# Attention stage of an encoder trunk: the bias kept as loaded, the far probabilities' parts moved forward, the weights' and keys' parts moved between the two heads' copies of values

## The chip, the cores and the metric

The kernel runs on one core of a Trainium2 chip. A core has five engines that run their own instruction streams and meet at semaphores: TensorE (PE in the profile, its weight loads PEld), VectorE (DVE), ScalarE (ACT), GpSimd (POOL) and SyncE (SP, which here only issues DMAs). Products of TensorE land in PSUM, eight banks of 512 f32 columns by 128 partitions; everything else lives in SBUF, 128 partitions wide. The metric is the device time of one execution in microseconds, taken as the median of several runs. Lower is better.

## The reference

One layer over 1024 tokens of width 1024, all in f32. What matters here is the attention between the input projection and the output projection:

```python
hn = rmsnorm(h, norm_mix_g[i])
z = hn @ w_in[i]
u = z[..., :POOL_W]                          # 512 columns for the pooling mixer
q, k, v = jnp.split(z[..., POOL_W:], 3, axis=-1)   # 8 heads of 64
a = pool_mixer(u, pool_w[i], pool_b[i], pool_scale[i])
o = chunk_attention(q, k, v, rel_bias[i])
h = h + jnp.concatenate([a, o], axis=-1) @ w_out[i]

# chunk_attention, for each chunk of 64 tokens: own chunk and the 8 before it
s = jnp.einsum('bqhd,bkhd->bhqk', qb, kb).astype(jnp.float32) * scale + bias
s = jnp.where(valid[None, None, None, :], s, -jnp.inf)
pr = jax.nn.softmax(s, axis=-1).astype(vb.dtype)
return jnp.einsum('bhqk,bkhd->bqhd', pr, vb)
```

After it come a gated MLP with a causal convolution, a gated per-layer embedding and a final norm; the change does not touch them.

## The kernel before

TensorE's fast format holds fewer bits than f32, so each f32 matrix is split into a high part (rounded, written by ACT: `act.activation(hi, src, AF.Copy)`) and a low part (what is left, written mostly by DVE: `src - hi`), and each product is three matmuls: high by high, high by low, low by high (`mm3`, lines 136 to 138). Whatever TensorE multiplies must first have gone through ACT and then DVE or POOL.

**Units.** The attention is cut into units: one pair of heads and one tile of 128 query tokens, except that the first three tiles go together. Four pairs by six units make 24 units (`UNITS`, numbered u). A query tile sees at most five key tiles. `unit(u)` issues the work of a unit in this order:

- `probs_t(u - 1)`: TensorE turns the probabilities of the unit before (L421) into PSUM banks 2 and 3; what does not fit there goes to banks 6 and 7. The parts of banks 2 and 3 are the near ones, those of 6 and 7 the far ones (`far = bank > 3`).
- `scores(u)`: queries by keys (L398) into banks 4 to 7.
- some steps of the projections (`fill`): 24 matmuls in all for a block of 128 columns, half the tokens and all eight slices of depth, three for each step. They keep TensorE busy while the other engines do the softmax. They make the next pair's queries and keys and, after those, the columns of the pooling mixer.
- `values(u - 1)`, if that unit closed one of the groups of tiles 0 to 2, 3 to 5 and 6 to 7: probabilities by values (L473) for both heads of the pair, in 12, 24 and 24 matmuls. With a group of three tiles each head has a PSUM bank of its own (bank 5 and the projection's free bank); with the group of two both heads share one. ACT then copies a half of each head's result (L476) and DVE adds the other half (L479). A unit with such a call is called valued.

**The order on ACT and DVE** is written out by hand through a list. `push(t, f)` puts a piece of work on the list with a due time in microseconds from the unit's start; `flush()` sorts the list by due time and issues everything. Both engines then run their instructions in the order issued. The due times that matter here: near high part 0.0, first reduction (L363, L367: scores plus bias, and the row's extreme) 1.0 and 1.8, exponentials (L375) 1.9 and 2.75, near low part 2.5 in a valued unit and 3.7 otherwise, reciprocals (L378) about 2.95 to 3.5, far high part 3.5, scalings (L373 on DVE, L371 on ACT) 3.0 to 4.0, far low part 3.55 or 4.4, the copy-out of a finished projection (L279, L559) when its matmuls are issued, at 3.6 at the earliest in a unit that is not valued. At 4.8 and later come the parts of the next pair's keys and queries (`lay`, L308 to L312) and of the projections' weights (`split_later`, L504 and L502; some low parts go to POOL).

```python
            flush()
            if u:
                values(u - 1)
```

So before the change all of a unit's work is issued before its products with the values are copied out. The weights go through two buffers of raw f32 (`load`, L190) and three slots of parts; the last block's two halves have places of their own. The first of the output projection's raw weights are loaded (L615) into the same raw buffers, each as soon as the input weights there have been split.

**The bias** of a head is a 128 by 640 tile, loaded (L348) into one of three buffers while the pair before is worked on. The queries carry the factor -1/8, so that a row's minimum is wanted, and the bias is negated by ACT after it has landed (L351); POOL then fills two corners with a large number that masks keys outside the band (L352, L353).

After the last unit come the rest of the projection, the output weights' parts and the parts of the attention's result (L141 and L142 through `split`), then the output projection and the mixer. ACT's and DVE's instructions of this part have an order of their own, and the program merges the two orders by its own estimate of when each is ready.

Of the kernel before, what the change touches and what calls it, by code (L numbers as in the profile page):

```python
# [11 lines left out]
P = 128  # L12
# [89 lines left out]
def trunk(tc, xT, pT, vecs, w_qk0, w_in, w_v, bias, counts, pool_w, w_out, w_up, w_down,  # L102
# [4 lines left out]
    with tc.tile_pool(name="sb", bufs=1) as sb, \  # L107
# [175 lines left out]

        def push(t, *fns):

            for n, fn in enumerate(fns):
                pending.append((t + 0.8 * n, len(pending), fn))

        def flush():
            todo = sorted(pending, key=lambda p: p[:2])  # L290
            pending.clear()
            owed.clear()
            for _, _, fn in todo:
                fn()


        def lay(c, x, h):

            z = slice(h * 512, (h + 1) * 512)

            def last(fn):
                fn()
                laid.add((c, x, h))

            src = qk32[x][:, z]
            if x:
                hi, lo = [a[:, z] for a in K[c % 2]]
                return [lambda: act.activation(hi, src, AF.Copy),  # L308
                        lambda: last(lambda: dve.tensor_tensor(lo, src, rv(hi), ALU.subtract))]
            hi, lo = [a[:, z] for a in Q]  # L310
            return [lambda: act.activation(hi, src, AF.Copy, scale=-0.125),
                    lambda: last(lambda: dve.scalar_tensor_tensor(lo, src, -0.125, rv(hi), ALU.mult, ALU.subtract))]  # L312

# [32 lines left out]
        def load_bias(h):  # L346
# [3 lines left out]
            def turned():  # L350
                act.activation(b, b, AF.Copy, scale=-1.0)  # L351
                pool.memset(b[0:64, 576:640], BIG)  # L352
                pool.memset(b[64:128, 0:64], BIG)  # L353
            return turned

        def softmax(todo, valued):

            for i, (x, b, ps, S, s_) in enumerate(todo):
                z = 2 * i / len(todo)

                def least(b=b, ps=ps, S=S, s_=s_):
                    if len(ps.shape) == 3:
                        dve.tensor_tensor_reduce(  # L363
                            S.rearrange("p (a b) -> p a b", a=2), ps,
                            b.rearrange("p (a b) -> p a b", a=2), 1.0, BIG, ALU.add, ALU.min, s_[:, 0:1])
                    else:
                        dve.tensor_tensor_reduce(S, ps, b, 1.0, BIG, ALU.add, ALU.min, s_[:, 0:1])  # L367

# [65 lines left out]
        def probs_out(todo, valued):  # L434
            for a, b, bank, ps in todo:
                src = ps.rearrange("p a (n q) -> p n a q", q=HD)
                hi, lo = [pt[:, a:b].rearrange("p k x (a q) -> p (k x) a q", a=2) for pt in PT]
                far = bank > 3
                push(3.5 if far else 0.0, lambda hi=hi, src=src: act.activation(hi, src, AF.Copy))
                push((3.55 if valued else 4.4) if far else 2.5 if valued else 3.7,  # L440
                     lambda lo=lo, src=src, hi=hi: dve.tensor_tensor(lo, src, rv(hi), ALU.subtract))
# [3 lines left out]
        def values(u):  # L445
# [6 lines left out]
            while u < NU - 1 and at[0] < 2.3:  # L452
                next(fill)
                credit -= 0.5
                now[0] += STEP
            flush()
            reach = {k: (max(t0, k), min(t1, k + BANDT)) for k in range(max(0, t0 - 4), t1)}
# [17 lines left out]
            for j in range(2):  # L475
                act.activation(otmp[halves[j], 0:n * P], Os[j][halves[1 - j]], AF.Copy)  # L476
            for j in range(2):
                a = halves[j]
                dve.tensor_tensor(o32[a, c_, t0 * P:t1 * P], Os[j][a], otmp[a, 0:n * P], ALU.add)  # L479

# [16 lines left out]
        def split_later(parts):  # L497

            t = max(5.2, now[0] + 0.4)
            for i, (name, src, hi, lo) in enumerate(parts):  # L500
                def low(name=name, src=src, hi=hi, lo=lo):
                    (pool if name[0] in (4 + 1, 8 + 2, 4 + 2, 8 + 3, 2) else dve).tensor_tensor(lo, src, rv(hi), ALU.subtract)  # L502
                    there.add(name)
                push(t + 0.7 * i, lambda src=src, hi=hi: act.activation(hi, src, AF.Copy))  # L504
                push(t + 0.8 + 0.7 * i, low)

# [140 lines left out]
        def lay_due(u):  # L647

            for c, x, h in list(qk_ready):
                if u >= (c - 1) * PER + (0 if x else PER - 1 if h else 1):  # L650
                    qk_ready.remove((c, x, h))
                    push(max(4.8, now[0] + 0.4), *lay(c, x, h))

# [3 lines left out]
        def unit(u):  # L657
# [33 lines left out]
            else:  # L691
                for _ in range(DRAIN):
                    now[0] += STEP
                    next(fill)
            flush()
            if u:
                values(u - 1)
            if turns and (u % PER == PER - 1 or u % PER == 1):
# [767 lines left out]
```

## Time and profile before

| | |
|---|---|
| time, median of 3 runs | 1122.74 us (1122.15 to 1123.06) |
| time of the profiled execution | 1122.08 us |
| its span, first to last instruction | 1120.3 us |
| busy: PE, DVE, ACT, POOL | 99%, 76%, 52%, 15% |
| mean granted clock of TensorE | 0.998 |
| attention stage | about 80 to 262 us |

Times in the profile are counted from the span's start. A row of the timeline has the start, the length, the engine, the line, the operation, what it writes and reads, its shape, how many like it are joined, and in brackets the idle time of its engine just before it with what ended it. A matmul's length in such a row includes its way through the array: matmuls of 512 columns start 0.23 us apart and are shown as 0.39 us long.

### The profile page before, as it was taken

What the parts mean: (1) busy time and instruction counts of PE and PEld (TensorE: products, weight loads), DVE (VectorE), ACT (ScalarE), POOL (GpSimd) and SP (SyncE); (2) the same over time, 40 slices, a digit from 0 to 9 for tenths busy, and PEclk for the clock granted to TensorE, in tenths of its full rate; (3) what the DMA queues carried; (4) which work ended last, traced back from release to release, by engine and by line L of the source; (5) the groups of instructions that cost most, each with busy time, mean ns of one, the idle gap of its engine ahead of it and who ended that gap; (6) DMA issues with size and microseconds to landing.
All of it is one profiled execution on the core that took longest, in us unless ns stands there. A gap on an engine that the chain in (4) does not pass through costs nothing.

```text
span 1120.3 us, 15614 instructions
## 1 busy us (share of the span) xinstructions
PE 1108.7 (99%) x5674; PEld 921.3 (82%) x5674; DVE 850.7 (76%) x1438; ACT 581.7 (52%) x1006; POOL 167.9 (15%) x212
## 2 busy tenths in 40 slices
PE   9999999999999999999999999999999999999997
PEld 7888888888888888888888888888888888888887
DVE  7537777778578878887787878777877789986845
ACT  8336777765665545443443444344544444674634
POOL 0000101186013200220121012201120112000000
PEclk9999999999999999999999999999999999999999
DMA  8100111104600452764567456756575556420003
GB/s 308 50 1 20 62 43 39 51 16 136 197 29 1 109 155 95 164 156 140 150 160 168 133 160 151 172 138 160 142 174 145 137 156 140 132 94 20 1 34 117
DMA packets 64878, 124.83 MB, mean 111 GB/s; under 512 B 7329, under 2 KB 8737, under 8 KB 64801
## 3 DMA queue, kind: packets, MB, share of 16 engines
q1 hardware_dynamic: 50688, 98.33, 26.8%
q0 software_dynamic: 13824, 25.17, 14.2%
q8 instruction: 44, 0.72, 0.3%
q10 hardware_dynamic: 288, 0.33, 0.1%
q14 instruction: 34, 0.27, 0.1%
HBM read 109.13 MB, written 14.68 MB: 111 GB/s over the span
## 4 chain that ended last, share of the span: by engine, by line
PE 65%; DVE 3%; issue 2%; ACT 1%; POOL 1%; POOLq 0%; DVEq 0%; ACTq 0%
PE PS L136 21%; PE PS L137 21%; PE PS L138 21%; DVE R L142 1%; ACT R L141 1%; POOL TB L925 0%; POOL F L915 0%; DVE F L907 0%; DVE F L1191 0%; ACT TB L896 0%; PE PS L778 0%; POOL small L782 0%; ACT F L770 0%; DVE TB L918 0%; DVE TB L919 0%
## 5 line engine op out<-in xcount | busy, mean ns | idle before, releaser
L136 PE MATMUL PS<-R 128*128 128x512 f32 (+1 forms) x1088 | 422.2, 388 | 0.2
L137 PE MATMUL PS<-R 128*128 128x512 f32 (+1 forms) x1088 | 418.7, 385 | 0.0
L138 PE MATMUL PS<-R 128*128 128x512 f32 (+1 forms) x1088 | 418.5, 385 | 0.0
L136 PEld LDWEIGHTS PS<-R 128*128 128x128 f32 x1088 | 204.6, 188 | 44.6 <-issue 2.9
L138 PEld LDWEIGHTS PS<-R 128*128 128x128 f32 x1088 | 204.5, 188 | 41.3
L137 PEld LDWEIGHTS PS<-R 128*128 128x128 f32 x1088 | 204.6, 188 | 39.8 <-DVE R L249 0.2
L141 ACT ACTIVATE R<-F 128x512 fp32r<-128x512 f32 (+2 forms) x221 | 137.4, 636 | 177.1 <-PE PS L137 85.6
L142 DVE TENSOR_TENSOR R<-F,R 128x512 fp32r<-128x512 f32 (+2 forms) x221 | 154.5, 713 | 49.7 <-ACT R L141 49.0
L1160 DVE TENSOR_TENSOR F<-F,PS 128x512 f32<-128x512 f32 x140 | 92.6, 681 | 6.8 <-PE PS L138 6.5
L850 DVE TENSOR_TENSOR F<-F 128x512 f32<-128x512 f32 x88 | 60.5, 688 | 44.8 <-DMA F<-in_w_up 42.1
L141 ACT ACTIVATE BQ<-RW 128x512 fp32r<-128x512 f32 x90 | 52.6, 622 | 80.4 <-PE PS L137 76.3
L1103 POOL DMA_DIRECT2D RW<-Yd x56 | 49.5, 889 | 264.4 <-DMA RW<-Yd 200.8
L1103 POOL DMA_DIRECT2D RW<-in_w_down x40 | 36.5, 966 | 228.7 <-DMA RW<-in_w_down 191.1
L142 DVE TENSOR_TENSOR BQ<-RW,BQ 128x512 fp32r<-128x512 f32 x90 | 59.1, 684 | 2.6 <-PE PS L137 2.2
L137 PE MATMUL PS<-BQ 128*128 128x512 f32 x140 | 54.6, 390 | 0.1
L136 PE MATMUL PS<-R,BQ 128*128 128x512 f32 x140 | 54.5, 389 | 0.0
L138 PE MATMUL PS<-R,BQ 128*128 128x512 f32 x140 | 54.5, 389 | 0.0
L136 PE MATMUL PS<-BQ 128*128 128x512 f32 x140 | 54.5, 389 | 0.0
L137 PE MATMUL PS<-R,BQ 128*128 128x512 f32 x140 | 54.5, 389 | 0.0
L138 PE MATMUL PS<-BQ 128*128 128x512 f32 x140 | 54.5, 389 | 0.0
L986 ACT ACTIVATE F<-F,vec 128x1024 f32<-128x1024 f32 (+1 forms) x25 | 28.6, 1143 | 44.1 <-DVE F L961 41.9
L375 ACT ACTIVATE F<-F,small 128x640 f32<-128x640 f32 (+4 forms) x64 | 44.0, 689 | 14.0 <-DVE small L363 12.6
(177 smaller groups left out, 1589.7 us busy)
## 6 DMA issues: line engine op xcount, KB each, us to landing
F<-in_w_up SPq DMA_DIRECT2D x91, 256.0 KB, 4.3
RW<-Yd SPq DMA_DIRECT2D x60, 256.0 KB, 3.8
RW<-Yd POOLq DMA_DIRECT2D x56, 256.0 KB, 4.9
RW<-in_w_down SPq DMA_DIRECT2D x50, 256.0 KB, 2.9
RW<-in_w_down POOLq DMA_DIRECT2D x40, 256.0 KB, 6.6
Yd<-F SPq DMA_DIRECT2D x40, 256.0 KB, 3.1
F<-in_w_in SPq DMA_DIRECT2D x10, 512.0 KB, 3.5
F<-in_xT SPq DMA_DIRECT2D x16, 256.0 KB, 5.4
```

Of the source, the lines that this page charges most:

```text
L136: pe.matmul(ps, ahi, bhi, start=first, stop=False, skip_group_check=more)
L137: pe.matmul(ps, ahi, blo, start=False, stop=False, skip_group_check=more)
L138: pe.matmul(ps, alo, bhi, start=False, stop=last, skip_group_check=more)
L141: both = (act.activation(hi, src, AF.Copy), dve.tensor_tensor(lo, src, rv(hi), ALU.subtract))
L142: dve.tensor_tensor(lo, src, rv(hi), ALU.subtract))
L375: push(1.9 + 0.85 * z, lambda S=S, s_=s_: act.activation(S, S, AF.Exp, bias=s_[:, 0:1], scale=-1.0, accum_out=s_[:, 1:2]))
L850: return dve.tensor_tensor(rawu[to], rawu[a], rawu[b], op)
L986: act.activation(y, Gb[:, 2 + a:2 + b], AF.Identity, bias=vec[:, C_CB + fi:C_CB + fi + 1], scale=cw(2))
L1103: pool.dma_start(t, src, accum_op=ALU.add)
L1160: dve.tensor_tensor(t, t, PS[:, 4 + d], ALU.subtract if n in (1, 5) else ALU.add)
```

## The change

Four things are done:

- The queries carry +1/8, the reduction multiplies by -1, and the bias stays as loaded. The negations on ACT (L351) are gone. The two corners are filled by DVE and with the opposite sign; POOL no longer takes part.
- The far high part is due at 0.05 and not 3.5, so behind the near high part; the far low part is due right behind the near low part (2.52 in a valued unit, 3.57 otherwise), which puts it ahead of reciprocals and scalings in a valued unit and ahead of the projection's copy-out in the others.
- Work of `split_later` and `lay_due` is marked slow. In a valued unit the list is first issued without the slow work (`flush(True)`), then come the products with the values. For a group of three tiles the slow work is issued between the first head's copy and addition and the second's. For the group of two it is issued after both.
- For a group of three tiles the order copy, copy, addition, addition becomes copy, addition, (slow work,) copy, addition on the list; for the group of two it stays.

```diff
@@ -281,17 +281,17 @@
         laid = set()
         pending, now, owed = [], [0.0], set()
 
-        def push(t, *fns):
+        def push(t, *fns, slow=False):
 
             for n, fn in enumerate(fns):
-                pending.append((t + 0.8 * n, len(pending), fn))
-
-        def flush():
-            todo = sorted(pending, key=lambda p: p[:2])
-            pending.clear()
+                pending.append((t + 0.8 * n, len(pending), fn, slow))
+
+        def flush(part=False):
+            todo = sorted((p for p in pending if not (part and p[3])), key=lambda p: p[:2])
+            pending[:] = [p for p in pending if part and p[3]]
             owed.clear()
-            for _, _, fn in todo:
-                fn()
+            for p in todo:
+                p[2]()
 
 
         def lay(c, x, h):
@@ -308,8 +308,8 @@
                 return [lambda: act.activation(hi, src, AF.Copy),
                         lambda: last(lambda: dve.tensor_tensor(lo, src, rv(hi), ALU.subtract))]
             hi, lo = [a[:, z] for a in Q]
-            return [lambda: act.activation(hi, src, AF.Copy, scale=-0.125),
-                    lambda: last(lambda: dve.scalar_tensor_tensor(lo, src, -0.125, rv(hi), ALU.mult, ALU.subtract))]
+            return [lambda: act.activation(hi, src, AF.Copy, scale=0.125),
+                    lambda: last(lambda: dve.scalar_tensor_tensor(lo, src, 0.125, rv(hi), ALU.mult, ALU.subtract))]
 
         later, tail = [], []
 
@@ -348,9 +348,8 @@
             sp.dma_start(b, bias[h])
 
             def turned():
-                act.activation(b, b, AF.Copy, scale=-1.0)
-                pool.memset(b[0:64, 576:640], BIG)
-                pool.memset(b[64:128, 0:64], BIG)
+                dve.memset(b[0:64, 576:640], -BIG)
+                dve.memset(b[64:128, 0:64], -BIG)
             return turned
 
         def softmax(todo, valued):
@@ -362,9 +361,9 @@
                     if len(ps.shape) == 3:
                         dve.tensor_tensor_reduce(
                             S.rearrange("p (a b) -> p a b", a=2), ps,
-                            b.rearrange("p (a b) -> p a b", a=2), 1.0, BIG, ALU.add, ALU.min, s_[:, 0:1])
+                            b.rearrange("p (a b) -> p a b", a=2), -1.0, BIG, ALU.add, ALU.min, s_[:, 0:1])
                     else:
-                        dve.tensor_tensor_reduce(S, ps, b, 1.0, BIG, ALU.add, ALU.min, s_[:, 0:1])
+                        dve.tensor_tensor_reduce(S, ps, b, -1.0, BIG, ALU.add, ALU.min, s_[:, 0:1])
 
                 def scaled(x=x, S=S, s_=s_):
                     if x:
@@ -436,8 +435,8 @@
                 src = ps.rearrange("p a (n q) -> p n a q", q=HD)
                 hi, lo = [pt[:, a:b].rearrange("p k x (a q) -> p (k x) a q", a=2) for pt in PT]
                 far = bank > 3
-                push(3.5 if far else 0.0, lambda hi=hi, src=src: act.activation(hi, src, AF.Copy))
-                push((3.55 if valued else 4.4) if far else 2.5 if valued else 3.7,
+                push(0.05 if far else 0.0, lambda hi=hi, src=src: act.activation(hi, src, AF.Copy))
+                push((2.5 if valued else 3.55) + 0.02 * far,
                      lambda lo=lo, src=src, hi=hi: dve.tensor_tensor(lo, src, rv(hi), ALU.subtract))
 
         credit, turns, valued = 0.0, [], [False]
@@ -453,7 +452,7 @@
                 next(fill)
                 credit -= 0.5
                 now[0] += STEP
-            flush()
+            flush(True)
             reach = {k: (max(t0, k), min(t1, k + BANDT)) for k in range(max(0, t0 - 4), t1)}
             wide = [k for k, (a, b) in reach.items() if b - a == n]
             narrow = sorted((k for k in reach if k not in wide), key=lambda k: reach[k][1] - reach[k][0])
@@ -473,10 +472,15 @@
                     pe.matmul(Os[j][:, (a - t0) * P:(b - t0) * P].rearrange("p (t q) -> p t q", q=P), V[:, k, 2 * c_ + j],
                               PT[part][:, b0:b0 + by * (b - a - 1) + 1:by, j], start=n_ == 0, stop=n_ == len(todo) - 1)
             for j in range(2):
-                act.activation(otmp[halves[j], 0:n * P], Os[j][halves[1 - j]], AF.Copy)
-            for j in range(2):
                 a = halves[j]
-                dve.tensor_tensor(o32[a, c_, t0 * P:t1 * P], Os[j][a], otmp[a, 0:n * P], ALU.add)
+                act.activation(otmp[a, 0:n * P], Os[j][halves[1 - j]], AF.Copy)
+                if n == 2 and j == 0:
+                    continue
+                for i in range(2) if n == 2 else (j,):
+                    a = halves[i]
+                    dve.tensor_tensor(o32[a, c_, t0 * P:t1 * P], Os[i][a], otmp[a, 0:n * P], ALU.add)
+                if j == 0:
+                    flush()
 
         nw = [0]
         bankn = [0]
@@ -501,8 +505,8 @@
                 def low(name=name, src=src, hi=hi, lo=lo):
                     (pool if name[0] in (4 + 1, 8 + 2, 4 + 2, 8 + 3, 2) else dve).tensor_tensor(lo, src, rv(hi), ALU.subtract)
                     there.add(name)
-                push(t + 0.7 * i, lambda src=src, hi=hi: act.activation(hi, src, AF.Copy))
-                push(t + 0.8 + 0.7 * i, low)
+                push(t + 0.7 * i, lambda src=src, hi=hi: act.activation(hi, src, AF.Copy), slow=True)
+                push(t + 0.8 + 0.7 * i, low, slow=True)
 
         def weights(ct, half):
 
@@ -649,7 +653,7 @@
             for c, x, h in list(qk_ready):
                 if u >= (c - 1) * PER + (0 if x else PER - 1 if h else 1):
                     qk_ready.remove((c, x, h))
-                    push(max(4.8, now[0] + 0.4), *lay(c, x, h))
+                    push(max(4.8, now[0] + 0.4), *lay(c, x, h), slow=True)
 
         for h in range(3):
             load_bias(h)()
@@ -692,9 +696,10 @@
                 for _ in range(DRAIN):
                     now[0] += STEP
                     next(fill)
+            if valued[0]:
+                flush(True)
+                values(u - 1)
             flush()
-            if u:
-                values(u - 1)
             if turns and (u % PER == PER - 1 or u % PER == 1):
                 turns.pop(0)()
             run_later(LATER)
```

## The prediction

> **What bounds the kernel now.** I read the page first, then the instructions of TensorE in order of time through the attention stage (80 to 262 us), then those of ScalarE (ACT) and VectorE (DVE) beside them.
>
> ```profile
> span 1120.3 us, 15614 instructions
> ...
> PE   9999999999999999999999999999999999999997
> ...
> PEclk9999999999999999999999999999999999999999
> ```
>
> TensorE is busy in all 40 slices at the full granted clock, so the time is TensorE's own stream plus the places where that stream stands still. This change touches no matmul and, as I follow the planner, not their order either. It can only remove or add standstills. These rows show the products with the values (L473), one call each; a row that goes on unbroken is a call without a wait, and in brackets stands what ended a wait.
>
> ```profile
> 85.89 1.79 PE L473 MATMUL PS<-B,R 128*128 128x384 f32 x12
> 149.07 3.66 PE L473 MATMUL PS<-B,R 128*128 128x384 f32 x24
> 166.78 2.96 PE L473 MATMUL PS<-B,R 128*128 128x256 f32 x24
> ...
> 104.06 1.33 PE L473 MATMUL PS<-B,R 128*128 128x384 f32 x7
> 105.68 2.70 PE L473 MATMUL PS<-B,R 128*128 128x128 f32 x17 [0.29 <-DVE B L441]
> 119.92 0.51 PE L473 MATMUL PS<-B,R 128*128 128x256 f32 x3
> 122.39 2.02 PE L473 MATMUL PS<-B,R 128*128 128x128 f32 x15 [0.46 <-DVE B L441]
> 195.07 1.32 PE L473 MATMUL PS<-B,R 128*128 128x384 f32 x7
> 196.68 2.71 PE L473 MATMUL PS<-B,R 128*128 128x128 f32 x17 [0.29 <-DVE B L441]
> 210.94 3.12 PE L473 MATMUL PS<-B,R 128*128 128x256 f32 x24
> 219.18 0.73 PE L473 MATMUL PS<-B,R 128*128 128x384 f32 x4
> 220.67 1.31 PE L473 MATMUL PS<-B,R 128*128 128x128 f32 x8 [0.76 <-DVE B L441]
> ...
> 159.04 0.92 PE L421 MATMUL PS<-ident,F 64*128 64x64 f32 x20 [0.33 <-DVE B L441]
> 249.65 0.59 PE L421 MATMUL PS<-ident,F 64*128 64x64 f32 x12 [0.46 <-DVE B L441]
> ```
>
> The first three rows are undisturbed calls of the three kinds: 1.79 us (tiles 0 to 2), 3.66 us (tiles 3 to 5), 2.96 us (tiles 6 and 7). Against them the call at 104.06 ends at 108.38, 4.32 us, so 0.66 us is lost; the one at 195.07 ends at 199.39, again 0.66 lost; 119.92 to 124.41 is 4.49 us, 1.53 lost; 210.94 loses 0.16; 219.18 to 221.98 is 2.80 us, 1.01 lost. Two runs of transposes (L421) waited 0.33 and 0.46 us. All of it together is 4.8 us, 0.4% of the time: more than that this change cannot give here.
>
> **The change part by part.**
>
> *Far parts behind near ones.* The probabilities of the last one or two key tiles (the far ones) come out as a high part on ACT (L439) and a low part on DVE (L441).
>
> ```profile
> 103.42 1.22 DVE L441 TENSOR_TENSOR B<-PS,B 128x1024 fp32r<-128x1024 f32 x1
> 105.20 0.42 DVE L441 TENSOR_TENSOR B<-PS,B 128x256 fp32r<-128x256 f32 x1
> L375 ACT ACTIVATE F<-F,small 128x640 f32<-128x640 f32 x32 | 26.3, 824 | 10.6 <-DVE small L363 10.6
> 219.06 0.96 DVE L373 TENSOR_SCALAR F<-F,small 128x512 f32<-128x512 f32 x1
> ```
>
> The wait of the call at 104.06 ended with the far low part, 105.20 to 105.62, which stood behind two reciprocals and a scaling. It now follows the near low part (103.42 to 104.64) directly and is done at about 105.0, when the products come to it (the eighth of 24, each 0.15 us: 104.06 + 1.0). The 0.66 goes, twice. The calls at 210.94 and 219.18 waited for the same part (in the latter case also behind the projection's copy-out): 0.16 and 1.01 go. At 159.04 and 249.65 the far low part stood behind a copy-out that now comes after it: 0.33 and 0.46 go. What the far high part costs ahead of the exponentials (0.36 us on ACT) is hidden: ACT idles 10.6 us before the 32 wide exponentials, two to a unit, 0.66 a unit, waiting for DVE; in the two tightest units about 0.1 us is left over, and falls on DVE work that has 0.3 us to spare. The scalings come 0.4 us later in units with values; the next transposes start two or more microseconds after them, but for the unit at 219, below.
>
> *Bias as loaded.* Eight negations leave ACT and sixteen fills move from POOL to DVE; the sign moves into constants that the reductions and the queries' parts carry already, at no cost.
>
> ```profile
> 117.64 0.29 DVE L367 CUSTOM_DVE_ANT_0 F<-PS,F 128x128 f32<-128x128 f32 x1 [1.07 <-POOL F L352]
> L219 DVE MEMSET B<- x1: 485/485/485, 0.9 to 0.9; 128x512 f32 x1
> ```
>
> The first row is where it pays: DVE stood 1.07 us for POOL's fill, which came behind the negation and behind a 1.28 us subtraction of a weight. With that gone, and the far part forward, the products at 119.92 find everything ready: the whole 1.53 goes. Of DVE fills the trace has one of 512 columns, 0.485 us; one of 64 costs between an eighth of it, 0.06, and the whole. I take 0.1, as the length goes with the columns in the copies too, so 0.2 us a head. The loads land before DVE comes to them, as the bias of heads 3 and 4 was asked for at 111 us and is filled at about 116.
>
> So the gains are 0.66 + 0.66 + 1.53 + 0.16 + 1.01 + 0.33 + 0.46 = 4.8 us.
>
> *Weights' and keys' parts between the copies of values.* Here the change adds waits. Before, these parts (ACT L504, L308, L311; low parts on DVE or POOL) ran while ACT had nothing to do but wait for the products. Now they are queued behind the copy L476 of the first head, which waits for the products, and ahead of that of the second.
>
> ```profile
> 176.92 0.62 ACT L504 ACTIVATE R<-F 128x512 fp32r<-128x512 f32 x1
> 177.91 0.49 ACT L476 ACTIVATE F<-PS 64x384 f32<-64x384 f32 x1 [0.38 <-PE PS L473]
> 178.73 0.48 ACT L476 ACTIVATE F<-PS 64x384 f32<-64x384 f32 x1 [0.33 <-PE PS L473]
> 180.31 0.82 DVE L363 CUSTOM_DVE_ANT_0 F<-PS,F 128x640 f32<-128x640 f32 x1 [0.50 <-PE PS L398]
> 183.02 1.21 DVE L441 TENSOR_TENSOR B<-PS,B 128x1024 fp32r<-128x1024 f32 x1
> 184.51 0.84 PE L421 MATMUL PS<-ident,F 64*128 64x64 f32 x20
> ```
>
> After the long calls (1.8 us from one head's copy to the other's) the parts fit between. After the short ones they do not. In this unit three copies of 0.52 each, start to start, now stand between 178.40 and the second copy: it begins at 180.1 and not 178.73. The addition and the two fills follow, and DVE's first reduction for the next tile starts at 181.35 instead of 180.31. That tile's chain (reduction, two exponentials, reciprocal, near low part 183.02 to 184.23) has only 0.28 us before the transposes at 184.51: TensorE waits 0.8 us. The unit at 131 us has two such copies, not three, so 0.5 less: 0.25. The one at 219 has one, but the unit before it now ends with its weight copy behind both value copies, so its chain runs 0.5 us late; the far part and the projection's copy-out (1.3 us together) now stand before its scaling too, which goes from 219.06 to about 220.05 and lasts 0.96 us beside POOL: 221.0. The products, freed of their wait, end at 220.74: the transposes wait 0.3. The first head's copy comes behind ACT's scaling, its addition ends at 221.9, and the scores want that bank at 221.55: 0.35 more. So 0.65 here. The unit at 86 us has one copy and 0.8 us of slack: nothing. Sum 1.7; between 0.5 (if fills and additions overlap what I put behind each other) and 2.5 (a second copy's 0.5 more in two units).
>
> The loads of input weights (L190) are issued when a weight's low part frees their buffer, so they too go up to 2.5 us later; each is first split more than a unit (6 us) after it has landed, so nothing waits.
>
> After tiles 6 and 7 both copies come first and the parts after them. That is harmless where the weights are needed a unit later, and only pushes the next unit's first copies back by 0.5 us (counted above where it tells). In the last call they are needed at once:
>
> ```profile
> 251.40 0.63 ACT L504 ACTIVATE B<-F 128x512 fp32r<-128x512 f32 x1
> 255.35 0.68 DVE L502 TENSOR_TENSOR B<-F,B 128x512 fp32r<-128x512 f32 x1
> 256.05 0.33 SPq L615 DMA_DIRECT2D F<-in_w_out  x1
> 256.44 2.96 PE L473 MATMUL PS<-B,R 128*128 128x256 f32 x24
> 258.99 2.72 ACT L141 ACTIVATE R<-F 128x512 fp32r<-128x512 f32 x5 [5.16 <-DMA F<-in_w_out]
> 259.24 0.40 PE L136 MATMUL PS<-R,B 128*128 128x512 f32 x1
> 261.74 0.77 ACT L476 ACTIVATE F<-PS 64x256 f32<-64x256 f32 x2
> ...
> 169.77 0.77 ACT L476 ACTIVATE F<-PS 64x256 f32<-64x256 f32 x2 [2.72 <-PE PS L473]
> ...
> 264.54 0.85 DVE L479 TENSOR_TENSOR F<-PS,F 64x256 f32<-64x256 f32 x2
> 233.91 1.22 DVE L502 TENSOR_TENSOR B<-F,B 128x512 fp32r<-128x512 f32 x1
> ```
>
> The last half of the last projection's weights is made at 251.40 and 255.35, and TensorE uses it at 259.24, right behind the last products. Now it is flushed behind both copies of these products. Those can start 2.99 us after the call begins (169.77 against 166.78), so at 259.43; they take 0.77, the weight's high part 0.63 more: 260.85, where TensorE wanted it at 259.24, 1.6 us. The low part follows on DVE behind two additions (0.85) and the high part, and takes 0.68 us, or 1.22 as at 233.91 if POOL is busy beside it: 261.7 to 262.2, while the third matmul wants it at 261.4: 0.3 to 0.8 more. I take 2.2 (1.9 to 2.4), nearer to the slow row since POOL is still pooling there. Zero is the lower end, if ACT's order differs from what I read. The load of the next output weights (256.05, issued when the weight's low part freed its buffer) moves to 262 too, and with it the five copies that begin at 258.99: they and their low parts (4.95 us on DVE before, behind them the pooled parts) come some 3.5 us late against TensorE. By my reading of DVE's queue up to 287 us the mixer's last product still finds its parts with 0.5 us to spare.
>
> Behind 262 us nothing removes what is left; TensorE's stream runs on without a gap, so it goes into the time whole. Sum: 4.8 gained, 1.7 and 2.2 lost, net 0.9. The profiled execution took 1122.08 us (span 1120.3 and 1.8 around it), 0.66 under the median of 1122.74; the same subtraction from the median gives **1121.8 us**.
>
> One question remains, whether a standstill of 2.2 us costs the clock too.
>
> ```profile
> 1.49 3.78 PE L221 MATMUL PS<-B 128*128 128x512 f32 x8 [1.49 <-DVE B L219]
> ```
>
> The first eight matmuls take 3.78 us where later ones of that size follow every 0.23 us, though the page rounds that slice to full clock; no wait in the attention stage, the longest 0.76 us, lowered it. I take no loss. The Trainium skill, "TensorE: Matmul & The Clock Gate", section "What's actually happening", has the clock fall to half after an idle window of about 3.4 us; by that 2.2 us of standstill is too short and the sum stays 1121.8, while the 3.9 us of the fourth rival below would be long enough. No run here shows such a fall.
>
> **The rivals.**
>
> *The last wait is hidden (17%).* If the last weight's parts land ahead of the products' copies, only the 1.7 is lost: 1122.7 - 3.1 = 1119.6. For it: before, copies of later work (258.99) stand between earlier ones, so the order on ACT is not purely the written one. Against: that is a merge of two lists, and inside the first the copies come first.
>
> *No part waits (5%).* All 4.8 are kept: 1117.9. Against it, the 0.28 us of slack at 184.51.
>
> *The late chain reaches the mixer (12%).* The weight loads, five copies and their low parts take more than the 0.5 us to spare; a load that takes 1 to 2 us longer gives 1122.8 to 1123.8.
>
> *The five copies stay ahead (7%), slower.* If ACT keeps 258.99's five copies in front, the value copies end at 262.51, the weight's high part at 263.15, the additions at 265.39, its low part at 266.1. TensorE stands 3.9 and then 2.5 us, 6.4 instead of 2.2: 1126.0, slower than before by 3.3. It decides as soon as the last wait passes 3.1 us. Against it: the first of the five needs a load into the buffer that this very weight occupies. If the clock then also fell, 2 us more (the first eight matmuls' 3.78 against 8 x 0.23).
>
> **How the numbers follow.** The sum holds within 1120.4 and 1122.8 with 55%; clock and what I have not seen get 4%. 0.2% (2.25 us) is about what a measurement of this kernel can tell from no change. The likeliest case lies within it, as does the late chain: same 0.65. Faster takes the first two rivals and the fast end of the sum, 0.26; slower the last rival and the rest, 0.09. The range, 1119.0 to 1124.3, takes in the hidden last wait below and the late chain above.
>
> **What would show it.** Right: calls of 3.66, 2.96 and 1.79 us throughout; no wait of DVE for POOL's fill near 117; transposes waiting 0.2 to 0.8 us after the short calls of the second and third head pair; a wait of TensorE of 1.9 to 2.4 us, ended by L504's and L502's writes, behind the last products. Wrong: no wait there, or one of over 3 us; transposes at 184 on time; new waits of the mixer's products.

## The result and the profile after

The changed kernel takes 1130.17 us (median of 6 runs, 1128.84 to 1130.91), the kernel before 1122.16 on the same chip (6 runs, 1121.73 to 1123.06): ratio 1.0068, 95% interval 1.0055 to 1.0081. It is 8.0 us slower, where 0.9 less was forecast. The profiled execution took 1130.05 us, span 1128.3. From the page of the kernel after, its span and the row of the granted clock (the row of TensorE's busy share reads as before):

```profile
span 1128.3 us, 15594 instructions
...
PEclk9999999999999999999999999999999999999998
```

At this scale next to nothing has changed, which is why the stage has to be opened. TensorE in order of time, the rows that answer to those of the prediction (line numbers have moved by a few: L472 are the products with the values, L420 the transposes, L362 and L366 the reductions, L438 and L440 the high and low parts of the probabilities, L508 and L506 those of the weights, L476 the copies of values, L481 their additions):

```profile
86.53 2.18 PE L472 MATMUL PS<-B,R 128*128 128x384 f32 x12
101.22 0.92 PE L420 MATMUL PS<-ident,F 64*128 64x64 f32 x20 [0.62 <-DVE B L440]
105.85 4.09 PE L472 MATMUL PS<-B,R 128*128 128x384 f32 x24
121.77 2.96 PE L472 MATMUL PS<-B,R 128*128 128x256 f32 x24
130.53 2.12 PE L472 MATMUL PS<-B,R 128*128 128x384 f32 x12
139.41 0.84 PE L420 MATMUL PS<-ident,F 64*128 64x64 f32 x20 [0.42 <-DVE B L440]
146.34 0.92 PE L420 MATMUL PS<-ident,F 64*128 64x64 f32 x20 [0.84 <-DVE B L440]
...
170.27 3.03 PE L472 MATMUL PS<-B,R 128*128 128x256 f32 x24 [0.93 <-ACT F L370]
188.97 0.84 PE L420 MATMUL PS<-ident,F 64*128 64x64 f32 x20 [0.83 <-DVE B L440]
195.37 0.92 PE L420 MATMUL PS<-ident,F 64*128 64x64 f32 x20 [0.33 <-DVE B L440]
```

The call at 121.77 is clean (2.96 us; before, 4.49): that gain came. The calls at 86.53 and 130.53, clean before, now take 2.18 and 2.12 in place of 1.79. The waits at 139.41 and 188.97 are the forecast ones; those at 101.22, 146.34 and 195.37 are new and stand where no part between copies can have made them. The transposes wait for the near low part each time, so it is the chain ahead of it that is late. What that chain waits for stands in the groups of VectorE's instructions from 84 to 262 us (busy time and mean | idle time just before them and what ended it), first of the kernel before, then after, and in its total of waits after (us, times, longest):

```profile
L363 DVE CUSTOM_DVE_ANT_0 F<-PS,F 128x640 f32<-128x640 f32 (+1 forms) x38 | 29.0, 801 | 10.3 <-PE PS L398 9.9
```

```profile
L362 DVE CUSTOM_DVE_ANT_0 F<-PS,F 128x640 f32<-128x640 f32 (+1 forms) x39 | 29.7, 799 | 17.1 <-ACT B L438 16.6 <-PE PS L397 0.5
...
DVE F L362 <- ACT B L438: 16.6, 15, 2.0
```

Before, the reduction waited for the scores on TensorE. Now it waits, 15 times, for the high parts on ACT, and 6.8 us longer in all. One unit of each, ACT and VectorE in order of time, before and after:

```profile
100.33 1.03 ACT L439 ACTIVATE B<-PS 128x1024 fp32r<-128x1024 f32 x1 [0.84 <-PE PS L421]
101.32 0.82 DVE L363 CUSTOM_DVE_ANT_0 F<-PS,F 128x640 f32<-128x640 f32 x1 [1.77 <-PE PS L398]
102.19 0.83 ACT L375 ACTIVATE F<-F,small 128x640 f32<-128x640 f32 x1 [0.83 <-DVE small L363]
```

```profile
102.12 1.38 ACT L438 ACTIVATE B<-PS 128x1024 fp32r<-128x1024 f32 x2 [0.69 <-PE PS L420]
103.53 0.82 DVE L362 CUSTOM_DVE_ANT_0 F<-PS,F 128x640 f32<-128x640 f32 x1 [2.04 <-ACT B L438]
104.40 0.83 ACT L374 ACTIVATE F<-F,small 128x640 f32<-128x640 f32 x1 [0.90 <-DVE small L362]
```

Near and far copy now follow each other (102.12 to 103.50), and the reduction starts 0.03 us after the far one ends: 1.41 us after the near copy began, where it was 0.99. So it is 0.42 us late against the near copy, and the exponentials with it. In the unit before, that distance grew from 0.39 us to 1.31, by 0.92. The reduction takes no data from this copy. They have the banks in common: by the code the far parts lie in banks 6 and 7 beside the scores (`place`: bank 6 from column 512 down), and a tile of over three key tiles has its scores in banks 4 + x and 6 + x. The compiled order of VectorE's instructions, with what each waits for, shows this bank by bank for the unit of three short tiles at 118 us. Its 128- and 256-wide scores lie in banks 4 and 5, its 384-wide ones in 6 and 7:

```
L366 ISA F,small<-PS,F 128x128 [waits DVE_49,PE_49]
...
L366 ISA F,small<-PS,F 128x256
...
L366 ISA F,small<-PS,F 128x384 [waits Activation_49]
```

Of these only the 384-wide one, on the far copy's banks, waits for ACT. The wait is one for ACT's semaphore, so it is written into the compiled program; what the banks would do without it, no run here shows. The Trainium skill, "PSUM — Partial Sum Buffer", section "PSUM bank collisions raise a hardware error", says that a compiler back end adds a dependency between any two instructions of different engines on one bank and quadrant, reads of ACT and VectorE included; these waits agree with it, and the prediction had not used it.

Behind the last products stands the wait that was forecast:

```profile
261.78 2.96 PE L472 MATMUL PS<-B,R 128*128 128x256 f32 x24
266.25 0.50 PE L136 MATMUL PS<-R,B 128*128 128x512 f32 x1 [1.51 <-ACT B L508]
267.34 0.50 PE L138 MATMUL PS<-R,B 128*128 128x512 f32 x1 [0.36 <-DVE B L506]
...
264.77 0.77 ACT L476 ACTIVATE F<-PS 64x256 f32<-64x256 f32 x2 [2.85 <-PE PS L472]
265.57 0.63 ACT L508 ACTIVATE B<-F 128x512 fp32r<-128x512 f32 x1
...
266.46 0.82 DVE L506 TENSOR_TENSOR B<-F,B 128x512 fp32r<-128x512 f32 x1
...
268.00:270.00 2.00, 2.00 (x11) 1.62 (x10) 0.00 (x0) 0.13 (x1) 1.82 (x3) 1.00 0.50 131
```

The first of these matmuls starts 4.47 us after the call of the last products, before 2.80, so it is 1.67 us late. The third starts 1.09 us after the first, before 0.46: 0.63 more, 2.3 us in all (2.4 by the fourth, as the first step behind a wait is 0.33 us and not 0.23). The last row is a window of two microseconds right behind; the third number from its end is the granted clock, which stayed at 1.00.

How the 8.0 us come about: the last products start at 261.78, before at 256.44, 5.3 later, of which 0.6 stood already at the stage's first call (86.53 against 85.89). So the stage from first to last call became 4.70 us longer (175.25 against 170.55), where the forecast had 3.1 less. Behind it come 2.4 for the wait just shown and 0.4 for one more, far on in the MLP: the matmul at 693.14 starts 0.64 us behind its forerunner and not 0.23, and waits for ACT's L942. The profiles of the kernel before and of tail_full below have no such wait, that of late_whole has one at 395, so it seems to come and go with the execution. The 0.6 ahead of the stage is within the spread of that start, which lies between 85.76 and 87.64 in the traces of this study.

In what follows each kernel's stage is this length from its own trace, against 170.55. It leaves out most of what differs from run to run: two pairs of kernels whose stages are the same program, the change and tail_full, and late_between and late_tail, agree in it within 0.01 us.

### The profile page after: what moved, and what is told of

Read it like the earlier page. It is cut to its first block, busy times and chain, and to the rows that moved or that the text cites. A ratio compares the mean times of both kernels' runs of the same rounds, so it can differ in the third digit from the quotient of the medians.

```text
span 1128.3 us, 15594 instructions
## 1 busy us (share of the span) xinstructions
PE 1112.0 (99%) x5674; PEld 922.2 (82%) x5674; DVE 850.4 (75%) x1454; ACT 577.3 (51%) x998; POOL 163.9 (15%) x196
## 4 chain that ended last, share of the span: by engine, by line
PE 83%; DVE 7%; ACT 5%; issue 3%; POOL 1%; DMA 0%; SPq 0%; POOLq 0%; DVEq 0%; ACTq 0%
PE PS L136 26%; PE PS L137 26%; PE PS L138 26%; PE PS L472 2%; DVE B L440 2%; ACT F L374 2%; ACT B L438 1%; DVE F L362 1%; DVE R L142 1%; PE PS L420 1%; PE PS L397 1%; DMA F<-in_xT 0%; ACT R L141 0%; POOL TB L930 0%; POOL F L920 0%
```

## The experiments

Theory: the far high copy, issued ahead of the reductions, makes them wait, and the chain behind them costs most of the 8.9 us that the forecast missed. Rival A: the parts between the copies of values are far dearer than 1.7 us. Rival B: the last wait goes on into the mixer. Times are medians; the ratio is to the kernel before, timed beside each on the same chip, and kernels not timed together are compared by their ratios.

**Far parts alone, and all but them.** far_alone takes from the change only these lines; far_back is the change with them undone.

```diff
-push(3.5 if far else 0.0, lambda ...high...)
-push((3.55 if valued else 4.4) if far else 2.5 if valued else 3.7, lambda ...low...)
+push(0.05 if far else 0.0, lambda ...high...)
+push((2.5 if valued else 3.55) + 0.02 * far, lambda ...low...)
```

> The kernel before (1122.2 us) with the far parts moved and nothing else. Theory: the reductions wait 0.4 to 1.4 us more in every unit with far parts: 1122.2 + 8.0 (all that was measured) - 2.2 (the last wait) - 1.7 (copies between) + about 1 (the fill) = about 1127 us (1125 to 1129). Rivals A and B: the far parts bring their gain of about 3.3 us, 1118.5 to 1119.5 us.

Measured: 1126.87 us, ratio 1.0038 (1.0025 to 1.0050), stage +4.35. The far parts by themselves make the kernel slower by 4.3 us, where they were to bring 3.3. VectorE's group shows the same wait as the change:

```profile
L363 DVE CUSTOM_DVE_ANT_0 F<-PS,F 128x640 f32<-128x640 f32 (+1 forms) x39 | 29.7, 799 | 18.9 <-ACT B L439 16.9 <-PE PS L398 2.0
```

Both rivals fall as the main cause.

> The changed kernel (1130.2 us) with the far parts back where they were, behind the exponentials; the bias, the split between the copies of values and the last wait stay. Theory (the far high copy on ACT, issued ahead of VectorE's two reductions, reads the same PSUM banks as they do, so they wait for it): the reductions wait for the scores alone again, the new waits of 0.2 to 0.9 us before the transposes go except after the short calls, the calls with values wait for the far low part as before, and the last wait stays: 1122.2 - about 1.1 (the fill) + 1.7 + 2.2 = about 1125.0 us (1124 to 1126.5). Rival A (the parts between the copies of values are much dearer than the 1.7 us forecast): the far parts gave their gain, so without them it is slower, 1131 to 1134 us. Rival B (the last wait carries on into the mixer): 1129 or more.

Measured: 1127.43 us (1125.87 to 1129.37), ratio 1.0046 (1.0033 to 1.0059), stage +1.55. The time is above the expected range and below rival A's; rival B's 1129 is not reached by the median, though two of the five runs reach it (1129.0 and 1129.37). The trace shows why the profiled run, 1127.42, lies so high: behind the last wait the clock fell. From the windows of that stretch (the last columns are the granted clock, the DMA share and GB/s) and from TensorE's rows:

```profile
264.00:266.00 2.00, 2.00 (x7) 1.57 (x7) 0.00 (x0) 0.00 (x0) 1.76 (x4) 0.67 0.46 131
266.00:268.00 2.00, 2.00 (x6) 1.52 (x6) 0.97 (x2) 1.64 (x4) 1.92 (x5) 0.50 0.00 0
...
264.82 0.63 PE L136 MATMUL PS<-R,B 128*128 128x512 f32 x1
265.25 0.63 PE L137 MATMUL PS<-R,B 128*128 128x512 f32 x1
...
268.17 0.39 PE L138 MATMUL PS<-R,B 128*128 128x512 f32 x1
268.39 0.39 PE L136 MATMUL PS<-R,B 128*128 128x512 f32 x1
```

Matmuls of 512 columns follow each other every 0.43 us from 264.82 to 267.81, then every 0.23 again; the clock row gives 0.33 x 2 + 0.50 x 2 = 1.7 us lost. Without it the run stands near 1125.7, inside the expected range, and close to the one run of the five whose mean granted clock is 0.998 (1125.87 us; the others have 0.996 or 0.997).

**The far high copy behind the reductions: a first try that missed.** far_behind is the change with one number altered, 0.05 to 2.8.

> The changed kernel with the far high copy issued behind both reductions and the exponentials (due 2.8 in place of 0.05), the far low part still right behind the near one, everything else as changed. Theory: the reductions find the scores at once, and the stage costs what the forecast said: 1130.2 - 8.4 = about 1121.8 us (1120.5 to 1124). Rivals A and B: the place of the high copy is of no weight, 1129 to 1131 us.

Measured: 1127.88 us, ratio 1.0047 (1.0034 to 1.0061), stage +3.13. The edit did more than it was meant to: in units with values the far low part is due 2.52, so it came ahead of the high part and subtracts an older one (the products are then not the layer's), and the high part, on the same banks, then waits for it. TensorE and ACT at the call near 105 us:

```profile
105.83 0.38 ACT L438 ACTIVATE B<-PS 128x256 fp32r<-128x256 f32 x1 [1.13 <-DVE small L377]
...
106.26 2.01 PE L472 MATMUL PS<-B,R 128*128 128x128 f32 x12 [1.10 <-ACT B L438]
```

The products waited 1.10 us for the high part. So it says nothing between theory and rivals; the next pair does.

**The same, in order.** far_mid issues it ahead of the low part, and takes the last wait out (in the last call, with u equal to NU, the slow work is now issued ahead of the products, as before the change):

```diff
-push(0.05 if far else 0.0, lambda ...high...)
+push((2.49 if valued else 2.8) if far else 0.0, lambda ...high...)
 ...
             if valued[0]:
-                flush(True)
+                flush(u < NU)
                 values(u - 1)
```

tail_full has the second edit alone.

> The changed kernel with the weights' parts flushed ahead of the copies of values in the last call alone, as before the change. Theory: TensorE's 1.67 and 0.53 us behind the last products go and nothing else: 1130.2 - 2.2 = 1128.0 us (1127.6 to 1128.4). Rival B (the late copies of the output weights cost more further on): 1125 to 1127 us. If the wait of 2.2 us were made up later it would stay 1130.

Measured: 1127.26 us (1126.96 to 1128.20), ratio 1.0042 (1.0029 to 1.0054), stage +4.69. That is 0.3 below the expected range. The ratios differ by 0.0026, 2.9 us, for a standstill of 2.4 and the 0.4 at 693 us that only the change's profile has; whether every run of the change had the second is not shown. Rival B has nothing left to explain.

> As tail_full (1127.3 us), with the far high copy behind the reductions: in units with values due 2.49, between the exponentials and ahead of the far low part, in the others due 2.8, behind the exponentials. Theory: no reduction waits for ACT, the calls with values find their far parts in time, and the stage ends some 1.6 us ahead of the kernel before (the 3.3 us of far gains and the 1.1 of the fill, less 2.2 to 2.8 for the copies between): 1121.0 us (1119.8 to 1123). Rival (the reductions' wait is not what costs; ACT's 0.36 us is): the copy stands ahead of an exponential still, 1125 to 1128 us.

Measured: 1120.26 us, ratio 0.9978 (0.9969 to 0.9986), stage -2.06. Against tail_full one due time has taken 7 us away, and the kernel is faster than before. The reductions wait 8.5 us in all, 8.2 of it for the scores and none for ACT. The theory's time was 0.7 too high; the rival falls.

**Between the two reductions.** far_between is tail_full with the copy due 1.05.

> As tail_full (1127.3 us), with the far high copy issued between the first and the second reduction (due 1.05). Theory (accesses of ACT and VectorE to one PSUM bank go in the order of issue): the first reduction waits for the scores alone, the copy waits for its end, and the second reduction waits for the copy, some 0.45 us, in every such unit; the first exponential is on time, the second late: 1124.5 us (1123 to 1126.5). Rival (the copy delays ACT, not VectorE): no reduction waits for ACT, and the time is that of tail_full within 0.5 us.

Measured: 1126.56 us, ratio 1.0036 (1.0023 to 1.0048), stage +4.08. The time lies between the two expectations and decides nothing; the trace does:

```profile
102.45 0.82 DVE L362 CUSTOM_DVE_ANT_0 F<-PS,F 128x640 f32<-128x640 f32 x1 [1.60 <-PE PS L397]
103.38 0.39 ACT L438 ACTIVATE B<-PS 128x256 fp32r<-128x256 f32 x1 [0.88 <-DVE small L362]
103.80 0.82 DVE L362 CUSTOM_DVE_ANT_0 F<-PS,F 128x640 f32<-128x640 f32 x1 [0.51 <-ACT B L438]
```

The first reduction waits for the scores again, the copy for the first reduction, the second reduction for the copy: here accesses of ACT and VectorE to one bank go in the order in which they are issued, one after the other. The wait is 0.51 us and only moved. That the time hardly falls fits a chain in which the second row's exponential counts, not the first's; no run separates the two.

**The bias alone.**

```diff
-                act.activation(b, b, AF.Copy, scale=-1.0)
-                pool.memset(b[0:64, 576:640], BIG)
-                pool.memset(b[64:128, 0:64], BIG)
+                dve.memset(b[0:64, 576:640], -BIG)
+                dve.memset(b[64:128, 0:64], -BIG)
 ... (the reductions' factor 1.0 to -1.0, the queries' -0.125 to 0.125)
```

> The kernel before (1122.6 us) with the bias as loaded and nothing else. Forecast: VectorE's wait of 1.07 us for POOL's fill goes, the call at 120 us still waits for its far low part: 0.7 to 1.1 us less, 1121.7 us (1121.3 to 1122). Rival (the fills on VectorE or the moved sign cost as much as they bring): 1122.6.

Measured: 1121.76 us, ratio 0.9992 (0.9983 to 1.0001), stage -0.58. VectorE goes from its fills into the reduction with no wait for POOL, and a fill takes 0.11 us:

```profile
117.28 0.11 DVE L351 MEMSET F<- 64x64 f32 x1
117.46 0.11 DVE L352 MEMSET F<- 64x64 f32 x1
117.60 0.29 DVE L366 CUSTOM_DVE_ANT_0 F<-PS,F 128x128 f32<-128x128 f32 x1
```

The kernel before took 1123.00 us beside it, so the gain is 1.2 us by the medians and 0.9 by the ratio, about as forecast, but the interval reaches 1. That it gains is shown by the trace, where the call at 120 us now loses 0.8 us and not 1.53, and not by the times.

**The copies between, and the last call.** late_whole, late_between and late_tail carry the bias and have the far parts behind the exponentials: high part due 2.8, low part due 2.82 in units with values and 3.57 in others. late_between and late_tail keep the split flush; late_tail alone keeps the change's last call. It is thus the whole change with nothing but the far parts placed anew.

```diff
 late_whole, far_mid_whole:
-            todo = sorted((p for p in pending if not (part and p[3])), key=...)
-            pending[:] = [p for p in pending if part and p[3]]
+            todo = sorted(pending, key=...)
+            pending.clear()
```

> As far_mid, with all pending parts flushed ahead of the copies of values in every call, as before the change (the weights' and keys' parts no longer stand between the two heads' copies). Theory: 1122.6 - 3.3 - 1.1 = about 1118.5 us (1117.5 to 1120), so the copies between cost 2 to 3 us by themselves. Rival (the forecast's 1.7 us for them is right): about 1119.3 if far_mid is 1121.0.

Measured: 1120.0 us, ratio 0.9974 (0.9965 to 0.9984), stage -2.90. 1.5 slower than expected: against far_mid the parts between cost 0.3 us by the medians and 0.84 in the stage, not 2 to 3, nearer to the rival's 1.7 than to the theory's but below both. With the far parts in their old places they do cost more: far_back's stage is 2.13 us longer than bias_alone's, and within the stage these two differ only in the parts between and the order of copies and additions.

> As far_mid_whole (1120.0 us), with the far high copy due 2.8 in every unit and, in units with values, the far low part due 2.82: behind both exponentials of two-row units and behind the fourth of the six short ones, where the copy stood on ACT for the last reduction for 0.57 us and the call with values began 0.93 us late. Theory: that wait goes and no other comes, 0.5 to 0.9 us less: 1119.3 us (1118.5 to 1120). Rival (the call waits for the projection's copy-out behind six reciprocals whatever ACT does): 1120.0.

Measured: 1120.27 us, ratio 0.9977 (0.9968 to 0.9986), stage -2.21. The wait did not go, so the theory of this step falls; the stage is even 0.7 longer than far_mid_whole's.

> As late_whole, with the weights' and keys' parts between the copies of values as in the change, but flushed whole in the last call. The forecast's 1.7 us for these parts: 1121.0 us. From far_mid against far_mid_whole (0.85 us over the stage): 1120.1. If they cost nothing: 1119.3.

Measured: 1121.10 us, ratio 0.9983 (0.9974 to 0.9991), stage -1.64. Against late_whole, timed beside it, the parts between cost 0.8 us by the medians and 0.57 in the stage. In the rows below, the first three are late_between's, the last is late_whole's:

```profile
L362 DVE CUSTOM_DVE_ANT_0 F<-PS,F 128x640 f32<-128x640 f32 (+1 forms) x39 | 29.7, 798 | 8.2 <-PE PS L397 7.9
...
166.71 3.03 PE L472 MATMUL PS<-B,R 128*128 128x256 f32 x24 [0.78 <-ACT F L370]
185.42 0.84 PE L420 MATMUL PS<-ident,F 64*128 64x64 f32 x20 [0.83 <-DVE B L440]
```

```profile
221.57 1.15 PE L397 MATMUL PS<-R 64*128 64x320 f32 x11 [0.61 <-DVE F L481]
```

The reductions wait 8.2 us, 7.9 of it for the scores and none for ACT, where the change had 17.1. The forecast waits of the parts between are there. Against a stretch without a wait, TensorE loses 0.9 us at 185 and 0.4 at 137, ahead of the transposes, 0.7 in the call at 219 and 0.5 behind it: 2.5 us. late_whole loses none of these, but 1.9 us at the scores: they wait for the first head's addition (L481), 1.03 us at 221, 0.61 near 131 and 0.22 near 88, since the parts then stand ahead of that head's copy. The kernel before and bias_alone have no such wait of the scores. It goes with the far low part, which now stands ahead of the reciprocals and so delays ACT's scaling: near 130 us the scaling begins 0.74 us before the call in bias_alone and 0.08 before it in late_whole, and the copies follow it. The split takes these waits away, which the forecast had not counted.

> As late_between, with the last call as changed (its weight's parts behind both copies): the whole change with the far high copy alone moved behind the reductions. Forecast's 2.2 us behind the last products: 1122.3 us if late_between is 1120.1, and no lowered clock. Rival (the standstill also drops the granted clock in some runs, as the profile of far_back shows at 265 us, 3.4 us at about half): single runs 1.7 to 2 us above that, median 1122.3 to 1124.2, spread over 2 us.

Measured: 1123.58 us (1122.24 to 1125.12), ratio 1.0008 (0.9999 to 1.0017), stage -1.65. The last call costs 2.5 us by the medians, and the profile shows 2.2 of standstill (1.67 and 0.51) and then the lowered clock, as the rival had it:

```profile
254.66 2.96 PE L472 MATMUL PS<-B,R 128*128 128x256 f32 x24
259.13 0.50 PE L136 MATMUL PS<-R,B 128*128 128x512 f32 x1 [1.51 <-ACT B L508]
260.10 0.50 PE L138 MATMUL PS<-R,B 128*128 128x512 f32 x1 [0.23 <-DVE B L506]
...
255.00:262.00 7.00, 5.26 (x30) 4.24 (x30) 1.54 (x3) 1.39 (x3) 6.53 (x11) 0.93 0.21 64
262.00:264.00 2.00, 2.00 (x6) 1.55 (x5) 0.67 (x1) 1.33 (x3) 1.76 (x4) 0.50 0.10 38
264.00:266.00 2.00, 2.00 (x9) 1.60 (x9) 2.00 (x4) 2.00 (x4) 1.92 (x3) 0.88 0.40 91
```

0.07 x 7 + 0.50 x 2 + 0.12 x 2 = 1.7 us lost. The times alone do not tell how many of the eleven runs had this. But the four slowest, 1123.87 (the profiled one) to 1125.12, are also the four with the lowest mean granted clock, 0.996 and 0.997 against 0.998 and 0.999, and they are 1.7 us slower on average than the other seven. That fits a fall in four of eleven; as the mean clock takes in the whole span, it does not prove it.

**The call at 166 us.** In far_mid, far_mid_whole and the three late kernels that call begins 0.93 us late. The view names ACT's scaling as releaser; but the copy-out of the projection, the last in VectorE's queue there (0.67 us from 165.89 in late_between), ends 0.15 us before the call, and it frees a bank. early_out is late_whole with it put ahead of the reciprocals:

```diff
-push(now[0] if valued[0] else max(now[0], 3.6), lambda: qk_out(x, h, ps))
+push(min(now[0], 2.9) if valued[0] else max(now[0], 3.6), lambda: qk_out(x, h, ps))
```

> As late_whole (1120.3 us), with the projection's copy-out (VectorE) in units with values due 2.9 at the latest, so right behind the far low part and ahead of the reciprocals and scalings; three calls change, among them the one near 166 us. Theory: that call's bank is freed by this copy-out, the last of VectorE's queue there, so its 0.93 us of wait goes: 1119.4 us (1118.9 to 1119.9). Rival (the wait is for ACT's scaling, the releaser that the view names, or comes back before the next transposes as the scalings are 0.67 us later): 1120.3 us.

Measured: 1119.66 us (1119.07 to 1120.33), ratio 0.9974 (0.9965 to 0.9984), stage -2.98:

```profile
164.40 0.68 DVE L279 TENSOR_TENSOR F<-PS,F 128x512 f32<-128x512 f32 x1
...
165.35 0.39 PE L138 MATMUL PS<-R,B 128*128 128x512 f32 x1
165.58 2.62 PE L472 MATMUL PS<-B,R 128*128 128x256 f32 x21
```

The call follows the projection unbroken: the copy-out it was. This is the fastest median of the study, but its ratio is that of far_mid_whole, and its interval overlaps those of far_mid_whole, late_whole and far_mid. That the wait goes is shown by the trace, and the stage is 0.77 shorter than late_whole's; that the kernel is faster than these is not shown by the times.

## Why the prediction was wrong, step by step

*TensorE bounds it, and only standstills change.* Right. All that moved the time are gaps in its stream (and the clock behind one of them).

*"What the far high part costs ahead of the exponentials (0.36 us on ACT) is hidden."* This is the step that failed. The 0.66 us a unit that ACT waits for VectorE was taken as cover. But the copy comes ahead of the reduction, which is what ACT waits for, and shares its banks. So 0.42 and 0.92 us fell on VectorE's chain in the two units measured; the prediction itself had found 0.28 us of slack behind that chain at 184.51. With the far high copy behind the reductions, the far low part behind it and all else as changed, 1130.17 becomes 1123.58 (by the ratios 6.7 us), and the stage goes from +4.70 to -1.65. The cover was looked for on the engine that does the moved work, not on the one queued behind it at the bank.

*The 4.8 us of gains.* The mechanism was right, seen once the copy is out of the way: the waits at 104, 159, 195, 211 and 249 are gone but for 0.1 us each at 104 and 195, and so is the 1.53 at 120. Of the 1.01 at 219, 0.69 stays in late_between and none in late_whole, so there it is the parts between that hold it. 0.93 is given back at 166, as the stream has gained more by then than the copy-out that frees the bank; "what is late next" was not asked there. Gains and losses together: forecast -3.1 for the stage, measured -1.65 with the copy placed right.

*Bias as loaded.* Right: no wait for POOL, 0.11 us a fill against 0.1; alone the time is 1.2 us less by the medians, 0.9 by the ratio, 0.58 in the stage.

*Weights' and keys' parts between the copies of values: 1.7 us.* The places were right: 0.9 and 0.4 at 185 and 137 (forecast 0.8 and 0.25), and about 219. What it comes to depends on where the far parts stand. In their old places it is 2.1 us (far_back against bias_alone, in the stage), more than forecast. Behind the exponentials it is 0.57 and 0.84 (late_between against late_whole, far_mid against far_mid_whole), less than forecast, as the moved far parts bring waits of the scores that the split takes away. That the two moves act on each other was left out of the sum.

*Last call: 2.2 us.* Right: 2.3 us, 1.67 and 0.63, in the change. That the late chain would not reach the mixer held as well: behind 268 us the next wait of TensorE in the profile is the one at 693, in the MLP. Of the rivals, the hidden last wait, the parts that do not wait and the five copies that stay ahead did not occur. The true cause was none of the four.

*No loss by the clock.* Held in the profiles of the change and of far_behind (granted 1.00 behind the wait), not in those of far_back and late_tail. So the term can be 0 or 1.7 us, and the prediction had a point where it needed a bound.

## What to carry to other kernels

Before moving a read of PSUM ahead of another engine's read, write down the banks of both: in this program those on one bank go in the order of issue, and whoever comes second waits out the first even where no data passes between them. Price a moved instruction on every engine that meets its banks, and put it where those accesses are done; here 0.05 against 2.49 or 2.8 is 7 us. After adding up gains, follow the earlier stream to the next bank or buffer it needs: what frees that has not become earlier by itself.

## What the runs showed of the hardware

The granted clock fell to about half after standstills of 2.3 us (1.67 and 0.67, far_back) and 2.2 us (1.67 and 0.51, late_tail). It stayed down for about 3.4 us, at a cost of 1.7 us. It did not fall in two other profiles with the same wait, the change's own (1.67 and 0.63) and far_behind's (1.67 and 0.50). The Trainium skill's idle window of about 3.4 us, which the prediction used ("TensorE: Matmul & The Clock Gate", "What's actually happening"), is thus no safe bound for a standstill here: the measurement shows the fall after less. The page also says that this window runs freely; then one standstill could fill enough of a window in one execution and be cut by its border in another. No run here shows the window itself, so why it comes in one execution and not in the next stays open.
